# One written list of items from the mixers' result to the second feed-forward, with two blocks 1024 columns wide

## The chip, the core and the metric

The kernel runs on one core of one Trainium2 chip. The metric is the device time in microseconds of one execution; the time of a kernel is the median of its runs. Beside the runs stands one profiled execution, from which every duration here is read.

## The reference

One layer on 256 positions of width 2048, in float32: a SwiGLU feed-forward, two mixers side by side, cross-attention into 256 memory positions with 4 heads of 512, and a second feed-forward. The part that matters here lies in the middle:

```python
y = jnp.concatenate([rms_norm(ya, out_norm_conv[l]), rms_norm(yb, out_norm_sgu[l])], axis=-1)
x = x + y @ w_mix_out[l]
h = rms_norm(x, xattn_norm[l])
mem_n = rms_norm(mem, mem_norm[l])
x = x + memory_cross_attention(h, mem_n, w_q[l], w_kv[l], w_o[l])
h = rms_norm(x, ffn2_norm[l])
x = x + MACARON_SCALE * swiglu_ffn(h, ffn2_w_in[l], ffn2_w_out[l])
```

Inside the attention, `q = h @ w_q`, the scores are `q @ k.T / sqrt(512)`, their softmax is multiplied by the values, and the four heads' outputs, joined, by `w_o`. `w_mix_out`, `w_q` and `w_o` are 2048 x 2048 each. Each residual sum is followed by an RMS norm, so the next product needs a sum of squares over all of `x`; the kernel leaves that factor to the end of the next product and applies only the gain beforehand.

## The kernel before

**Weights.** Every float32 weight is split into two halves of a shorter type. SP's queue loads a tile `raw` of 128 x 1024 (512 KB) from HBM; ScalarE casts it to the high half (L145), VectorE subtracts the high half from `raw` to get the low half (L146). Both halves go into one place `hl`. There are 4 raws (`wraw`) and 3 places (`whl`). TensorE then runs three matmuls for each product: high half of the activations by high half of the weights (L225), by the low half (L226), and low half of the activations by the high half (L227). One tile of weights gives 12 matmuls of 128 x 512.

**The middle, by `gemm_n` (L213).** The mixers' result, the queries and the attention's result are each computed in 4 blocks of 512 columns; a block takes 8 tiles of weights (of two rows of 128 each) and two accumulators. The first halves of the mixers' first two blocks stand earlier, beside the mixers; of the second halves each takes 4 tiles. In what order each engine runs these instructions is set by the framework's scheduler from the order in which the program issues them, with some places tied by hand (`tc.issue_after`).

**A block's way back.** A finished block holds tokens on partitions, but `x` is kept with features on partitions. `by_tokens` (L346) copies the two accumulators out on ScalarE (L350), VectorE transposes in squares of 32 (L388, in `sent`), GpSimd's queue writes the tile to HBM (L390) and, when that has landed, issues four reads back (L393). `arriving` (L353) gives two parts: the first adds the four blocks of features into `x` (`xT`, two additions at L360, which wait for the reads) and then makes, for two of them, the next product's activations with gain in both halves (ScalarE L327, VectorE L328) and the sum of squares (ScalarE L303, VectorE L304); the second part does the other two. The parts are put into a later block's loop over the weights by `between`.

**Heads.** `probabilities` (L1518) splits a head's keys and queries, multiplies them, and runs, for each half of the positions, a chain: maximum (VectorE L1531), scale (L1532), exponential with its sum (ScalarE L1535), reciprocal (VectorE L1536), scale (L1537). `turned` transposes the result on TensorE and splits it and the head's values; `attend` multiplies them into `o_hl`.

**The second feed-forward** is an object with a `Line` (L448): a list of `Item`s, each with a source, a place and a use. The engines' order there is the written one: after item s is used, its place is taken by the cast of the next item that lacks one, the subtract of the item before that one follows, and then the parts in the `post` list of item s run. `begin` is its first 16 items (window 1350.1 to 1394.1 us of the trace), with activations of the attention's residual; `x_turn` (L1630) transposes `x` into two buffers and `x_leaves` (L1638) writes those to HBM (1 MB each) for the end of the kernel; `give` (L785) ends a group of columns.

Of the kernel before, what the change touches and what calls it, by code (L numbers as in the profile page):

```python
# [62 lines left out]


# [32 lines left out]
def layer(ctx: ExitStack, tc: tile.TileContext, a: dict):  # L97
# [248 lines left out]
    def by_tokens(name, acc, flat, back, scales=None):  # L346

        o = flat.rearrange("p (q t n) -> p q t n", q=4, t=2)
        for t in range(2):
            nc.scalar.copy(out=o[:, :, t], in_=by_q(acc[t]))  # L350
        sent(name, flat, back)

# [32 lines left out]
    def sent(name, flat, back, q=None):  # L385

        q = q or nc.gpsimd
        nc.vector.transpose(out=flat, in_=flat)  # L388
        away = dram.tile([4, 32, 4, flat.shape[-1] // 4], F32, name=name)
        q.dma_start(out=away.rearrange("i b q n -> (i b) (q n)"), in_=flat)  # L390
        z = back.rearrange("p (i n) -> p i n", i=4)
        for i in range(4):
            q.dma_start(out=z[32 * i:32 * i + 32], in_=away[:, :, i].rearrange("i b n -> b i n"))  # L393
# [160 lines left out]

    class FeedForward:
# [6 lines left out]
        def __init__(self, stack, tags, name, x_hl, gain, w_in, w_out, patterns, sums, steps, out_s, late):  # L562
# [29 lines left out]
            self.line = Line(  # L592
                [Place(lambda: whl.tile([P, 2, 1024], F32R, name="hl")) for _ in range(3)], []
            )
# [4 lines left out]
        def spared(self):  # L599

            spare = big.tile([P, 8192], F32, name="spare", tag=self.tags[2])
            raws = [spare[:, i * 1024:(i + 1) * 1024] for i in range(6)]
            self.u = [spare[:, 6144 + i * 512:6144 + (i + 1) * 512] for i in range(4)]
            self.raws_summed = [raws.pop() for _ in range(2)]
            self.in_spare = self.fixed(raws)
            self.line.raws.extend([Place(lambda: wraw.tile([P, 1024], F32, name="raw")) for _ in range(4)] + self.in_spare)

        def ahead(self, rules):

            head, more = rules  # L610

            def most(s):
                for j, end in enumerate(self.ends):
                    if s <= end:
                        return min(end + more[j], s + head if j == 0 else 1 << 30)
                return 1 << 30
            return most
# [32 lines left out]
        def sides(self, i):  # L650

            k = 2 * self.spairs[i]
            xg = self.u[2 * (i % 2)].rearrange("p (k t) -> p k t", k=2)
            f = self.u[2 * (i % 2) + 1].rearrange("p (f n) -> p f n", f=4)
            a11, a21, a12, a22 = xg[:, 0, :P], xg[:, 0, P:], xg[:, 1, :P], xg[:, 1, P:]
            form = self.forms[i]

            def scaled():
                for q in range(2):
                    nc.scalar.activation(out=xg[:, q], in_=xT[:, k + q], func=AF.Copy, scale=self.gain(k + q))  # L660

            def summed():
                nc.vector.scalar_tensor_tensor(
# [8 lines left out]
            def parted():  # L672
                split(form[:, :, 0], form[:, :, 1], f)
# [138 lines left out]
        def group(self, j):  # L812
            b = {"begun": set()}
            parts = self.pairs(j, ORDERS.get(j, range(8)), lambda p: self.patterns[j][p] == "S", b)
            p1, u2, u4, u5 = self.u
            self.last_seven[1].now.append(lambda: self.joins_first(b, p1))
            self.last_seven[1].post.append(lambda: self.joins_sevens(b, p1, u2, u4, u5))
            parts[-1][-1].post += [
                lambda: self.joins_eights(b, p1, u2, u4, u5), lambda: self.give(j, (p1, u2), (u4, u5)),
# [158 lines left out]
    def given(ff):  # L978
# [3 lines left out]
        ff.in_x[0].until = ff.ends[NG - 1] - 14  # L982
# [4 lines left out]
    def groups(ff, items):  # L987


        for j in range(1, NG):  # L990
# [8 lines left out]
            if j == NG - 1:  # L999
# [4 lines left out]
                ff.in_ring[0].until = ff.in_ring[1].until = len(items) + flat.index(ff.last_seven[-1])  # L1004
            items += flat
            ff.ends.append(len(items))
        for place in ff.in_spare + ff.in_low:
            place.until = len(items) - 1
        return items

    with ExitStack() as stack:
# [165 lines left out]
        ff.in_high[0].until = rest["until_again"] = len(items) - 1  # L1177
# [27 lines left out]
    with ExitStack() as stack:  # L1205
        with tc.tile_pool(name="mix", bufs=1) as pool:
# [280 lines left out]
            x_hl = gained_tile("S1")  # L1487
            ss = st.tile([P, T], F32, name="ss", bufs=2)
            arrivals = []
            for n in range(4):  # L1490
                if n < 2:
                    acc = gemm_n(a["w_mix_out"][n], y_of, acc=accs[n], between=arrivals, after=0, ks=range(0, 8, 2), first=-1, last=7)
                else:
                    acc = gemm_n(a["w_mix_out"][n], y_of, between=arrivals, after=8)
                if n < 3:
                    flat = pool.tile([P, 4, 2, P], F32, name="o", tag="o", bufs=2).rearrange("p q t n -> p (q t n)")
                else:
                    flat = big.tile([P, 8192], F32, name="last_o", tag="S2")[:, :1024]
                by_tokens(f"x_away{n}", acc, flat, flat)
                arrivals += arriving(4 * n, flat, x_hl, "xattn_norm", ss)  # L1500


        with tc.tile_pool(name="attn", bufs=1) as pool:
            def queries(h, between=None, after=8, step=8):
                acc = gemm_n(a["w_q"][h], lambda k: x_hl[:, k], between=between, after=after, step=step)
                flat = pool.tile([P, 1024], F32, name="q", bufs=2)
                by_tokens(f"q_away{h}", acc, flat, flat)
                return flat

            def halves_by_feature(name, flat):  # L1510
                hl = pool.tile([P, KH, 2, T], F32R, name=name)
                z = flat.rearrange("p (i t k a) -> p i t k a", i=4, t=2, k=4)
                for t in range(2):
                    d = hl[:, :, :, t * P:(t + 1) * P].rearrange("p k two (i a) -> p k two i a", i=4)
                    split(d[:, :, 0], d[:, :, 1], z[:, :, t].rearrange("p i k a -> p k i a"))
                return hl

            def probabilities(h, q):  # L1518
                with tc.issue_after(newest_copy[0].ins):
                    k_hl = halves_by_feature("k_hl", kT[:, h])  # L1520
                    q_hl = halves_by_feature("q_hl", q)
                pr = []
                for t in range(2):
                    acc = pa.tile([P, 2, M], F32, name="aux")
                    s = slice(t * P, (t + 1) * P)
                    for d in range(KH):
                        product_joint(acc, q_hl[:, d, 0, s], q_hl[:, d, 1, s], k_hl[:, d], d == 0, d == KH - 1)
                    e = pool.tile([P, M], F32, name="e", bufs=4)
                    mx = st.tile([P, 1], F32, name="mx", bufs=2)
                    sm = st.tile([P, 1], F32, name="sum", bufs=2)  # L1530
                    nc.vector.reduce_max(out=mx, in_=acc[:, 0], axis=AX.X)  # L1531
                    nc.vector.tensor_scalar(  # L1532
                        out=mx, in0=mx, scalar1=r_t[:, t:t + 1], scalar2=-1.0, op0=ALU.mult, op1=ALU.mult
                    )
                    nc.scalar.activation(out=e, in_=acc[:, 0], func=AF.Exp, scale=r_t[:, t:t + 1], bias=mx, accum_out=sm)  # L1535
                    nc.vector.reciprocal(out=sm, in_=sm)  # L1536
                    nc.vector.tensor_scalar(out=e, in0=e, scalar1=sm, scalar2=None, op0=ALU.mult)  # L1537
                    pr.append(e)
                return pr

            def turned(h, pr):

                p_hl = pool.tile([P, 2, 2, T], F32R, name="p_hl")
                for m in range(2):
                    tp = pa.tile([P, 2, T], F32, name="aux")
                    for t in range(2):
                        state["turned"] = nc.tensor.transpose(
                            out=tp[:, 0, t * P:(t + 1) * P], in_=pr[t][:, m * P:(m + 1) * P], identity=ident
                        )
                    split(p_hl[:, m, 0], p_hl[:, m, 1], tp[:, 0])  # L1550
                v_hl = pool.tile([P, 2, 2, HD], F32R, name="v_hl", bufs=2)
                with tc.issue_after(newest_copy[0].ins):
                    split(v_hl[:, 0], v_hl[:, 1], vv[:, :, h * HD:(h + 1) * HD])
                return p_hl, v_hl

            def attend(h, p_hl, v_hl):
                for d in range(KH):
                    acc = ps.tile([P, 2, 256], F32, name="acc")
                    c = slice(d * P, (d + 1) * P)
                    for m in range(2):  # L1560
                        product_joint(acc, v_hl[:, 0, m, c], v_hl[:, 1, m, c], p_hl[:, m], m == 0, m == 1)
                    split(o_hl[:, h * KH + d, 0], o_hl[:, h * KH + d, 1], acc[:, 0])

            state = {}

# [345 lines left out]
```

## Time and profile before

| | |
|---|---|
| runs | 2050.7, 2053.42, 2051.87 us; median 2051.87 |
| profiled execution | 2049.72 us, of which the span from first to last instruction is 2047.9 |
| granted TensorE clock | 0.996 of full, mean of the span |
| TensorE, VectorE, ScalarE, GpSimd busy | 99%, 87%, 61%, 8% of the span |
| moved | 501.05 MB, mean 245 GB/s |
| the stretch that the change rewrites | from about 1071 us (second halves of the mixers' result) to 1394 us (end of `begin`) |

The busy share of TensorE is a mean over stages; its matmuls overlap, so a busy TensorE may still run below its full rate. A group's row gives busy time and mean of one instruction, then the idle time that stood ahead of it on its engine and what ended it. In a timeline's row the bracket at its end is that idle time. In a row of windows each engine has its busy time in the window and, in brackets, the number of instructions; then the granted clock, the share of time in which the DMA engines were busy, and GB/s.

### The profile page before, as it was taken

How to read it: one execution, taken by the hardware profiler on the slowest of the kernel's cores; microseconds unless marked ns; L12 is line 12 of the kernel's file. 1: busy time of each engine (PE TensorE's matmuls, PEld its weight loads, DVE VectorE, ACT ScalarE, POOL GpSimd, SP SyncE). 2: the span in 40 equal slices, each digit the busy share in tenths (PEclk: the TensorE clock that was granted, in tenths of full speed). 3: DMA queues.
4: the chain of work that ended last, by engine and by line, in shares of the span. 5: the costliest groups of instructions: out<-in, count | busy, mean ns of one | idle time of the engine just before them, and what ended most of it. 6: DMA issues, size and time to landing. Idle time of an engine off the chain costs nothing. (4 is left out here: it accounts for less than half of the span.)

```text
span 2047.9 us, 26059 instructions
## 1 busy us (share of the span) xinstructions
PE 2027.9 (99%) x9004; PEld 1673.6 (82%) x9004; DVE 1785.4 (87%) x2474; ACT 1250.3 (61%) x1605; POOL 157.2 (8%) x240
## 2 busy tenths in 40 slices
PE   9999999999999999999999999999999999999998
PEld 8888888888888888888888788777888888888886
DVE  7999999989898989999876666678999999988997
ACT  7666666656665654444655455556667666655555
POOL 0000000000110011011001110100000010000002
PEclk9999999999999999999999999999999999999999
DMA  9889888989676677677667665688888988896665
GB/s 353 269 257 278 269 272 260 279 250 285 216 265 223 214 255 219 207 232 236 197 199 245 213 204 165 200 270 298 263 265 257 285 269 265 237 304 202 206 221 180
DMA packets 149525, 501.05 MB, mean 245 GB/s; under 512 B 17936, under 2 KB 29840, under 8 KB 148752
## 3 DMA queue, kind: packets, MB, share of 16 engines
q1 hardware_dynamic: 129456, 432.64, 62.5%
q0 software_dynamic: 19360, 66.07, 15.0%
q8 instruction: 70, 1.15, 0.2%
q10 hardware_dynamic: 576, 0.66, 0.1%
q14 instruction: 63, 0.52, 0.1%
HBM read 472.05 MB, written 27.26 MB: 244 GB/s over the span
## 5 line engine op out<-in xcount | busy, mean ns | idle before, releaser
L145 ACT CAST hl<-raw 128x1024 fp32r<-128x1024 f32 x224 | 235.3, 1052 | 234.4 <-PE acc L227 176.5
L146 DVE TENSOR_TENSOR hl<-raw,hl 128x1024 fp32r<-128x1024 f32 x224 | 273.1, 1221 | 96.0 <-ACT hl L145 95.6
L513 ACT CAST hl<-raw 128x1024 fp32r<-128x1024 f32 (+1 forms) x132 | 129.7, 994 | 57.4 <-DVE raw L711 22.4
L488 DVE TENSOR_TENSOR hl<-raw,hl 128x1024 fp32r<-128x1024 f32 (+1 forms) x132 | 151.6, 1155 | 14.0 <-ACT hl L513 11.7
L226 PE MATMUL acc<-hl,x_hl 128*128 128x512 f32 x384 | 150.3, 391 | 0.0
L227 PE MATMUL acc<-hl,x_hl 128*128 128x512 f32 x384 | 149.1, 390 | 0.0
L225 PE MATMUL acc<-hl,x_hl 128*128 128x512 f32 x384 | 134.9, 390 | 1.0 <-ACT x_hl L327 1.0
L226 PE MATMUL acc<-hl,m_hl 128*128 128x512 f32 x256 | 100.6, 393 | 0.0
L227 PE MATMUL acc<-hl,m_hl 128*128 128x512 f32 x256 | 99.6, 389 | 0.0
L513 ACT CAST hl<-sums 128x1024 fp32r<-128x1024 f32 x50 | 52.7, 1053 | 63.2 <-DVE sums L708 57.7
L225 PE MATMUL acc<-hl,m_hl 128*128 128x512 f32 x256 | 90.0, 391 | 0.0
L225 PEld LDWEIGHTS acc<-hl,x_hl 128*128 128x128 f32 x384 | 72.0, 188 | 16.4 <-ACT x_hl L327 1.4
L227 PEld LDWEIGHTS acc<-hl,x_hl 128*128 128x128 f32 x384 | 72.1, 188 | 14.8 <-DVE x_hl L328 0.2
L226 PEld LDWEIGHTS acc<-hl,x_hl 128*128 128x128 f32 x384 | 72.1, 188 | 14.7
L417 PE MATMUL acc<-hl,x_hl 128*128 128x512 f32 x192 | 75.1, 391 | 0.8 <-DVE hl L488 0.6
L416 PE MATMUL acc<-hl,x_hl 128*128 128x512 f32 x192 | 74.9, 390 | 0.0
L417 PE MATMUL acc<-more,x_hl 128*128 128x512 f32 x184 | 71.6, 389 | 0.0
L416 PE MATMUL acc<-more,x_hl 128*128 128x512 f32 x184 | 71.6, 389 | 0.0
L647 POOL DMA_DIRECT2D hl_s<-in_ffn_w_in x36 | 31.7, 879 | 489.7 <-ACT hl_s L645 489.7
L513 ACT CAST hl<-raws_out 128x1024 fp32r<-128x1024 f32 (+1 forms) x53 | 51.9, 985 | 27.5 <-PE acc L419 8.6
L488 DVE TENSOR_TENSOR hl<-raws_out,hl 128x1024 fp32r<-128x1024 f32 (+1 forms) x53 | 61.3, 1159 | 8.0 <-ACT hl L513 7.1
L645 ACT ACTIVATE more<-spare 128x1024 fp32r<-128x1024 f32 x36 | 38.1, 1059 | 43.9 <-PE acc L417 43.9
(674 smaller groups left out, 6172.5 us busy)
## 6 DMA issues: line engine op xcount, KB each, us to landing
spare<-in_ffn_w_in SPq DMA_DIRECT2D x208, 512.0 KB, 6.8
raw<-in_ffn_w_in SPq DMA_DIRECT2D x143, 512.0 KB, 6.9
raw<-in_ffn_w_out SPq DMA_DIRECT2D x90, 512.0 KB, 5.1
raws_out<-in_ffn_w_out SPq DMA_DIRECT2D x68, 512.0 KB, 5.4
hl_s<-in_ffn_w_in POOLq DMA_DIRECT2D x36, 512.0 KB, 7.2
more<-in_ffn_w_in POOLq DMA_DIRECT2D x36, 512.0 KB, 7.5
raw<-in_w_mix_vg SPq DMA_DIRECT2D x32, 512.0 KB, 4.6
raw<-in_w_k SPq DMA_DIRECT2D x32, 512.0 KB, 4.4
```

Of the source, the lines that this page charges most:

```text
L145: newest_copy[0] = nc.scalar.copy(out=hl[:, 0, :size], in_=raw[:, :size])
L146: newest[0] = nc.vector.tensor_tensor(out=hl[:, 1, :size], in0=raw[:, :size], in1=hl[:, 0, :size].bitcast(F32), op=ALU.subtract)
L225: nc.tensor.matmul(acc[t], lhsT=x[:, 0, s], rhs=hi[:, k], start=k0 + k == first, stop=False)
L226: nc.tensor.matmul(acc[t], lhsT=x[:, 0, s], rhs=lo[:, k], start=False, stop=False)
L227: newest_matmul[0] = nc.tensor.matmul(acc[t], lhsT=x[:, 1, s], rhs=hi[:, k], start=False, stop=k0 + k == last)
L416: nc.tensor.matmul(acc[t][g], lhsT=x[:, 0, s], rhs=hi[:, cols[g]], start=(t, g) in first, stop=False)
L417: nc.tensor.matmul(acc[t][g], lhsT=x[:, 0, s], rhs=lo[:, cols[g]], start=False, stop=False)
L488: nc.vector.tensor_tensor(out=hl[:, 1, :n], in0=item.raw[:, :n], in1=hl[:, 0, :n].bitcast(F32), op=ALU.subtract)
L513: nc.scalar.copy(out=item.hl[:, 0, :item.n], in_=item.raw[:, :item.n])
L645: nc.scalar.activation(out=hl[:, 1], in_=raw, func=AF.Copy, scale=-1.0)
L647: nc.gpsimd.dma_start(out=hl[:, 1], in_=self.source(*self.sums_at[at]), accum_op=ALU.add)
```

## The change

The four matrices' work and the heads' steps become items of one `Line`, 88 of them, put ahead of the second feed-forward's items in the same list. Items 0 to 23 are the mixers' result (4, 4, 8 and 8 items for its blocks), 24 to 39 the first two heads' queries as one block 1024 wide with four accumulators, 40 to 55 the other two heads', 56 to 71 the first half of `w_o` 1024 wide, 72 to 87 its other two blocks. An item of a wide block reads one row of 128 by 1024 columns where a narrow one reads two by 512; both are 512 KB and 12 matmuls. The weights `w_q` and `w_o` are laid out for that before the launch.

The scheduler's order is replaced by the written one. Where a returning block is added stands at numbered items: `arrives` puts the first part behind one item and the second behind the next. The heads' steps stand in `HEAD_STEPS`, one row per head, one number per step (keys, queries, probabilities, values, turned, attend). The second feed-forward's object, with its 5 further places for weights, is made behind item 68; four raws in its spare buffer join behind item 87. In `begin` the last two blocks of `w_o` arrive behind its items 0, 1 and 7, 8 (before, only the last one came in `begin`, at 4 and 5); `x_turn` moves from items 6 to 13 to items 9 to 15, `x_leaves(0)` from 11 to 14. Half of `attend`'s accumulators come from the other PSUM pool.

```diff
+HEAD_STEPS = (
+    (45, 46, 47, 48, 50, 52),
+    (50, 51, 52, 53, 55, 57),
+    (55, 57, 58, 59, 61, 63),
+    (62, 63, 64, 65, 66, 67),
+)
...
-            arrivals = []
-            for n in range(4):
-                if n < 2:
-                    acc = gemm_n(a["w_mix_out"][n], y_of, acc=accs[n], between=arrivals, after=0, ks=range(0, 8, 2), first=-1, last=7)
-                else:
-                    acc = gemm_n(a["w_mix_out"][n], y_of, between=arrivals, after=8)
...
-                by_tokens(f"x_away{n}", acc, flat, flat)
-                arrivals += arriving(4 * n, flat, x_hl, "xattn_norm", ss)
+        line = Line(hl_places(), raw_places())
...
+        def wide(w, x_of, accs):
+
+            def use(k):
+                def go(hl):
+                    if not accs:
+                        accs.extend(bank(ps, "acc") for _ in range(4))
+                    x = x_of(k)
                     for t in range(2):
+                        s = slice(t * P, (t + 1) * P)
+                        for g in range(2):
+                            c = slice(g * G, (g + 1) * G)
+                            three(
+                                accs[2 * g + t], (x[:, 0, s], x[:, 1, s]), hl[:, 0, c], hl[:, 1, c], k == 0, k == KD - 1
+                            )
                 return go
+            return [fed(use(k), w[:, k]) for k in range(KD)]
...
+        def goes(name, items, accs, tile=flat_tile):
+            flats = state[name] = []
+            def copies():
+                for i in range(len(accs) // 2):
+                    flats.append(tile(i))
+                    o = flats[i].rearrange("p (q t n) -> p q t n", q=4, t=2)
+                    for t in range(2):
+                        nc.scalar.copy(out=o[:, :, t], in_=by_q(accs[2 * i + t]))
+            def through():
+                for i, away in [(i, leaving(f"{name}_{i}", flat)) for i, flat in enumerate(flats)]:
+                    returned(away, flats[i])
+            items[-1].now.append(copies)
+            items[-1].post.append(through)
+            return items
+        def arrives(at, f, name, i, norm):
+            parts = []
+            def go(q):
+                def part():
+                    if q == 0:
+                        parts.extend(arriving(f, state[name][i], state["x_hl"], norm, state["ss"]))
+                    parts[q]()
+                return part
+            for q in range(2):
+                at[q].post.append(go(q))
...
+        Q, W = 24, 56
+        for at, f, name in ((13, 0, "y_away0"), (18, 4, "y_away1"), (24, 8, "y_away2"), (32, 12, "y_away3")):
+            arrives(items[at:], f, name, 0, "xattn_norm")
+        for at, f, name, i in ((W + 23, 0, "a_away0", 0), (W + 26, 4, "a_away0", 1)):
+            arrives(items[at:], f, name, i, "ffn2_norm")
...
+        for h, steps in enumerate(HEAD_STEPS):
+            for at, part in zip(steps, (keys, asked, probabilities, values, turned, attend)):
+                items[at].post.append(lambda part=part, h=h: part(h))
+        def second():
+            attn.close()
...
-        after = {k: [lambda k=k: x_turn(k - 6)] for k in range(6, 14)}
-        after[4], after[5] = [arrivals[0]], [arrivals[1]]
-        after[11].append(x_leaves(0))
-        after[15] = [x_leaves(1)]
+            after = {k: [lambda k=k: x_turn(k - 9)] for k in range(9, KD)}
...
+            arrives(items, 8, "a_away1", 0, "ffn2_norm")
+            arrives(items[7:], 12, "a_away2", 0, "ffn2_norm")
+            items[14].post.append(x_leaves(0))
+            items[15].post += [lambda: x_turn(7), x_leaves(1)]
...
+        items[W + 12].post.append(second)
```

**How it moves instructions: the third block of the mixers' result on VectorE.** In these rows of VectorE's order `hl` is a tile of weights, `o` the finished block, `xT` the residual `x`. Before:

```order
L388 STREAM_TRANSPOSE o<-o 128x1024
L146 TENSOR_TENSOR hl<-raw,hl 128x1024 x4
L360 TENSOR_TENSOR xT<-xT,o 128x4x128 x2
L146 TENSOR_TENSOR hl<-raw,hl 128x1024
L328 SCALAR_TENSOR_TENSOR x_hl<-xT,pv,x_hl 128x256
L304 TENSOR_TENSOR ss<-ss,sq 128x256
```

After, where line numbers are higher (L496 is the subtract, L392 the transpose, L361 the addition, L336 and L312 the gain and the squares) and every finished block is called `flat`; the rows go from the third block's transpose to its addition, which is the last row but two, and the first addition among them is the second block's:

```order
L392 STREAM_TRANSPOSE flat<-flat 128x1024
L496 TENSOR_TENSOR hl<-raw,hl 128x1024 x3
L361 TENSOR_TENSOR xT<-xT,flat 128x4x128 x2
...
L496 TENSOR_TENSOR hl<-raw,hl 128x1024
...
L496 TENSOR_TENSOR hl<-raw,hl 128x1024 x4
L392 STREAM_TRANSPOSE flat<-flat 128x1024
L496 TENSOR_TENSOR hl<-raw,hl 128x1024
L361 TENSOR_TENSOR xT<-xT,flat 128x4x128 x2
L336 SCALAR_TENSOR_TENSOR x_hl<-xT,pv,x_hl 128x256
L312 TENSOR_TENSOR ss<-ss,sq 128x256
```

Between a block's transpose and its addition stood 4 subtracts; now there are 9, and the next block's transpose.

**The attention's result on VectorE.** Here `h` and `z` are the buffers that hold finished blocks of `w_o`, two each. Before, around the first two blocks:

```order
L388 STREAM_TRANSPOSE h<-h 128x1024
L146 TENSOR_TENSOR hl<-raw,hl 128x1024
L388 STREAM_TRANSPOSE h<-h 128x1024
L146 TENSOR_TENSOR hl<-raw,hl 128x1024 x4
L360 TENSOR_TENSOR xT<-xT,h 128x4x128 x2
L146 TENSOR_TENSOR hl<-raw,hl 128x1024
L328 SCALAR_TENSOR_TENSOR x_hl<-xT,pv,x_hl 128x256 x2
```

After; `ring`, `hl_l` and `hl_h` are the further places for weights:

```order
L392 STREAM_TRANSPOSE h<-h 128x1024 x2
L496 TENSOR_TENSOR hl<-raw,hl 128x1024 x3
L496 TENSOR_TENSOR ring<-raw,ring 128x1024 x2
L496 TENSOR_TENSOR hl_l_10369<-raw,hl_l_10369 128x1024
L496 TENSOR_TENSOR hl_l_10370<-raw,hl_l_10370 128x1024
L496 TENSOR_TENSOR hl_h<-raw,hl_h 128x1024
L392 STREAM_TRANSPOSE z<-z 128x1024
L361 TENSOR_TENSOR xT<-xT,h 128x4x128 x2
L336 SCALAR_TENSOR_TENSOR x_hl<-xT,pv,x_hl 128x256 x2
```

Where 4 subtracts stood between the second transpose and the first addition, there are now 8 and the third block's transpose.

**A head's softmax on VectorE.** `aux` are the scores, `mx` and `sum` their maximum and sum, `e` the probabilities. Before, from the second head's split queries:

```order
L154 TENSOR_TENSOR q_hl<-q,q_hl 128x4x128 x2
L146 TENSOR_TENSOR hl<-raw,hl 128x1024 x2
L388 STREAM_TRANSPOSE q<-q 128x1024
L146 TENSOR_TENSOR hl<-raw,hl 128x1024
L154 TENSOR_TENSOR o_hl<-acc,o_hl 128x256 x4
L1531 TENSOR_REDUCE mx<-aux 128x1 x2
L1532 TENSOR_SCALAR mx<-mx,r_t 128x1 x2
L1536 RECIPROCAL sum<-sum 128x1
L1537 TENSOR_SCALAR e<-e,sum 128x256
L1536 RECIPROCAL sum<-sum 128x1
L1537 TENSOR_SCALAR e<-e,sum 128x256
L146 TENSOR_TENSOR hl<-raw,hl 128x1024 x2
```

After, from the first head's:

```order
L162 TENSOR_TENSOR q_hl<-flat,q_hl 128x4x128 x2
L496 TENSOR_TENSOR hl<-raw,hl 128x1024
L392 STREAM_TRANSPOSE flat<-flat 128x1024
L1655 TENSOR_REDUCE mx<-aux 128x1
L1656 TENSOR_SCALAR mx<-mx,r_t 128x1
L1660 RECIPROCAL sum<-sum 128x1
L1661 TENSOR_SCALAR e<-e,sum 128x256
L1655 TENSOR_REDUCE mx<-aux 128x1
L1656 TENSOR_SCALAR mx<-mx,r_t 128x1
L1660 RECIPROCAL sum<-sum 128x1
L1661 TENSOR_SCALAR e<-e,sum 128x256
L496 TENSOR_TENSOR hl<-raw,hl 128x1024
```

The two halves' chains ran interleaved; now the second starts when the first has ended, and the next subtract stands behind both.

More of the change, by code (lines that the diff above doesn't have):

```diff
@@ L553, in run, with hl_places, raw_places, __init__ @@
                 last[i.engine] = i
+    def hl_places():
+        return [Place(lambda: whl.tile([P, 2, 1024], F32R, name="hl")) for _ in range(3)]
+    def raw_places():
+        return [Place(lambda: wraw.tile([P, 1024], F32, name="raw")) for _ in range(4)]
     class FeedForward:
-        def __init__(self, stack, tags, name, x_hl, gain, w_in, w_out, patterns, sums, steps, out_s, late):
+        def __init__(self, stack, tags, name, x_hl, gain, w_in, w_out, patterns, sums, steps, out_s, late, line=None):
             self.w_in, self.w_out, self.x_hl, self.gain = w_in, w_out, x_hl, gain
@@ L604, in spared @@
             self.raws_summed = [raws.pop() for _ in range(2)]
-            self.in_spare = self.fixed(raws)
-            self.line.raws.extend([Place(lambda: wraw.tile([P, 1024], F32, name="raw")) for _ in range(4)] + self.in_spare)
+            self.spare_raws = raws
+            self.line.raws.extend(self.in_spare)
         def ahead(self, rules):
@@ L612, in most @@
             def most(s):
+                s -= self.base
                 for j, end in enumerate(self.ends):
                     if s <= end:
[L615 removed]
+                        return self.base + min(end + more[j], s + head if j == 0 else 1 << 30)
                 return 1 << 30
@@ L1658, in layer @@
-        items = ff.begin(
-            lambda k: None, after, (r_x, inverse_root_parts(r_x, lambda: x_tot[0][:, 0, 0:2], 1.0 / D, RMS_EPS)), (0, 1, 2, 9),
-        )
-        items[14].post.append(lambda: given(ff))
-        groups(ff, items)
-        rest = {}
-        sums = st.tile([P, 2, 4], F32, name="sums")
-        st.tile([P, 136], F32, name="to_64_too")
-        most = [st.tile([P, 1], F32, name=f"f_most{t}") for t in range(2)]
-        def quarters(o):
-            return [o[:, t, g * G:(g + 1) * G] for g in range(2) for t in range(2)]
@@ L1765, in layer @@
-        items[ff.ends[NG - 1] - 5].post.append(raws_out)
-        items[ff.ends[NG - 1] - 1].post.append(ff.out_places)
-        parts, _, _ = ff.block(0, first_place, lambda o: None)
-        flat = [item for part in parts for item in part]
-        for i in range(6, 2 * NG):
-            flat[i - 6].post.append(ff.turn(i))
-        flat[1].post.append(lambda: ff.by_blocks(NG - 1))
-        flat[2].post.append(lambda: ff.leaves(NG - 1))
-        flat[16].post.append(hl_out)
-        items += flat
@@ new lines, in values, with turned @@
+        def values(h):
+            state["v"] = pool.tile([P, 2, 2, HD], F32R, name="v_hl")
+            split(state["v"][:, 0], state["v"][:, 1], vv[:, :, h * HD:(h + 1) * HD])
+        def turned(h):
+            pr, p_hl = state["p"], pool.tile([P, 2, 2, T], F32R, name="p_hl")
+            for m in range(2):
+                tp = pa.tile([P, 2, T], F32, name="aux")
+                for t in range(2):
+                    nc.tensor.transpose(
+                        out=tp[:, 0, t * P:(t + 1) * P], in_=pr[t][:, m * P:(m + 1) * P], identity=ident
+                    )
+                split(p_hl[:, m, 0], p_hl[:, m, 1], tp[:, 0])
+            state["p_hl"] = p_hl
@@ L1820, in layer @@
+        last = items[-1]
+        items[W + 12].post.append(second)
         line.add(items)
-        line.most = ff.ahead(AHEAD[1])
         line.run()
```

552 lines of the change are left out of this document (280 added, 272 removed).

## The prediction

> **What bounds the kernel now.** I read the page first, then the table of windows for the stretch that the change rewrites, the waits, and the timeline around each gap. The page's line of engines:
>
> ```profile
> PE 2027.9 (99%) x9004; PEld 1673.6 (82%) x9004; DVE 1785.4 (87%) x2474; ACT 1250.3 (61%) x1605; POOL 157.2 (8%) x240
> ```
>
> TensorE sets the time, so only its lost time can be won. The windows, cut where TensorE stood idle and where it didn't (columns: window, its length, PE, PEld, DVE, ACT, POOL busy with their counts, TensorE's clock, DMA share, GB/s):
>
> ```profile
> 1131.40:1138.40 7.00, 3.77 (x11) 2.67 (x10) 5.64 (x10) 4.31 (x10) 0.00 (x0) 0.77 0.25 74
> 1138.40:1158.00 19.60, 19.60 (x87) 16.24 (x86) 11.04 (x12) 8.87 (x10) 2.77 (x5) 1.00 0.84 257
> 1159.40:1316.00 156.60, 156.60 (x788) 133.00 (x789) 97.16 (x143) 82.98 (x128) 16.77 (x30) 1.00 0.65 197
> 1316.00:1323.50 7.50, 5.72 (x18) 4.23 (x17) 7.38 (x14) 6.05 (x14) 0.00 (x0) 0.77 0.39 107
> 1344.60:1350.10 5.50, 3.29 (x14) 2.07 (x12) 5.50 (x11) 4.67 (x10) 0.00 (x0) 1.00 0.31 95
> 1350.10:1394.10 44.00, 44.00 (x195) 36.32 (x196) 38.31 (x60) 25.86 (x39) 2.78 (x5) 1.00 0.88 305
> 1400.90:1408.20 7.30, 5.75 (x17) 3.71 (x16) 6.54 (x9) 5.33 (x7) 0.93 (x1) 0.77 0.75 164
> ```
>
> The second row gives the full rate: 19.60 / 87 = 0.2253 us a matmul, so an item of 12 takes 2.70. A gap's loss is its length less its matmuls at that rate: A (1131) 7.00 - 11 x 0.2253 = 4.5; C (1316) 7.50 - 18 x 0.2253 = 3.4; D (1345) 5.50 - 14 x 0.2253 = 2.3; F (1401) 7.30 - 17 x 0.2253 = 3.5. The waits of TensorE up to 1400 add a small one, B, in the queries' first block:
>
> ```profile
> PE acc L226 <- DVE hl L146: 6.6, 3, 3.2
> PE acc L225 <- ACT x_hl L327: 1.0, 1, 1.0
> PE acc L417 <- DVE hl L488: 0.6, 1, 0.6
> ```
>
> (total, times, longest.) So A to D cost 4.5 + 1.0 + 3.4 + 2.3 = 11.2, F another 3.5. TensorE waits for the subtract; the timelines of VectorE and TensorE at A show what that waited for:
>
> ```profile
> 1124.52 1.23 DVE L146 TENSOR_TENSOR hl<-raw,hl 128x1024 fp32r<-128x1024 f32 x1 [1.50 <-ACT hl L145]
> 1132.76 1.29 DVE L360 TENSOR_TENSOR xT<-xT,o 128x512 f32<-128x512 f32 x2 [7.01 <-DMA o<-x_away]
> 1133.97 1.22 DVE L146 TENSOR_TENSOR hl<-raw,hl 128x1024 fp32r<-128x1024 f32 x1
> 1131.39 0.61 PE L225 MATMUL acc<-hl,y_hl 128*128 128x512 f32 x2
> 1135.24 0.80 PE L226 MATMUL acc<-hl,y_hl 128*128 128x512 f32 x1 [3.23 <-DVE hl L146]
> 1135.84 0.63 PE L227 MATMUL acc<-hl,y_hl 128*128 128x512 f32 x1
> ```
>
> VectorE stood 7.01 us at an addition whose block had not come back, with the next subtract behind it; 1.2 us after that subtract began, TensorE went on, with wider spacing for a while. The same addition opens C, D, and, in `begin`, the backlog ahead of F:
>
> ```profile
> 1316.12 1.29 DVE L360 TENSOR_TENSOR xT<-xT,h 128x512 f32<-128x512 f32 x2 [5.56 <-DMA h<-o_away]
> 1344.11 1.29 DVE L360 TENSOR_TENSOR xT<-xT,z 128x512 f32<-128x512 f32 x2 [5.35 <-DMA z<-o_away]
> 1371.08 1.29 DVE L360 TENSOR_TENSOR xT<-xT,z 128x512 f32<-128x512 f32 x2 [4.90 <-DMA z<-o_away]
> ```
>
> **The change part by part.** An item is 12 matmuls of 128 x 512, one 512 KB load, one cast and one subtract in either form, so TensorE's work and the bytes stay; what can change is the gaps.
>
> *The returns come in time (gains A to D).* GpSimd's rows of the first write of a return, for A, C, D and the last block:
>
> ```profile
> 1117.54 0.56 POOL L390 DMA_DIRECT2D x_away<-o  x1 [15.92 <-DVE o L388]
> 1299.90 0.56 POOL L390 DMA_DIRECT2D o_away<-h  x1 [50.05 <-DVE h L388]
> 1329.90 0.56 POOL L390 DMA_DIRECT2D o_away<-z  x1 [15.27 <-DVE ss L304]
> 1353.52 0.56 POOL L390 DMA_DIRECT2D o_away<-z  x1 [15.13 <-DVE z L388]
> ```
>
> To the additions above these are 15.2, 16.2, 14.2 and 17.6 us. Only 4 subtracts stood between, some 4 x 2.70 = 10.8 us, which is why each addition waited. Now the distance from a block's last item to the item behind which it is added is 10, 11, 9 and 9 items for the mixers' result, 8 and 11 for the wide block of `w_o`, 9 and 8 for the narrow ones. From these go the copies out and the transpose:
>
> ```profile
> L350 ACT COPY q<-acc 128x512 f32<-128x512 f32 x8 | 4.6, 588 | 5.4 <-PE acc L227 5.1
> L388 DVE STREAM_TRANSPOSE q<-q 128x1024 f32<-128x1024 f32 x4 | 5.0, 1245 | 4.6 <-ACT q L350 4.6
> ```
>
> 2 x 0.59 + 1.25 and some handing over, 2.6 us. The shortest narrow allowance is 8 x 2.70 - 2.6 = 19.0. The wide one has two more copies ahead of its first write, so at worst 8 x 2.70 - 2.6 - 1.2 = 17.8, against 16.2 for the pair of blocks in C, and 17.6 is the longest return seen. Tight there, ample elsewhere. GpSimd's queue holds a second block's reads behind the first's as before. I take the whole 11.2; the bounds are nothing (all late again) and 11.2.
>
> The clock's part in these losses: TensorE's granted clock is 0.77 in A after 3.23 us idle, but also in C, after 7.50 - 5.72 = 1.8. The Trainium skill, TensorE: Matmul & The Clock Gate, Part 1, says that the clock falls to half after at least one idle window of about 3.4 us. By that page a gap would cost only its idle time, A to D 3.23 + 1.0 + 1.8 + 2.2 = 8.2 and F 1.55, the gain here would be some 4 smaller, near 2044; the rows of C and F, with clock 0.77 after under 2 us idle, disagree, and the measured losses stand.
>
> *The written order adds work between a tile's release and its subtract.* With 3 places, the subtract of item s+3 has from the end of item s to the end of s+2, 2 x 2.70 = 5.4 us, and what is posted behind item s stands ahead of it on VectorE. The rows:
>
> ```profile
> L146 DVE TENSOR_TENSOR hl<-raw,hl 128x1024 fp32r<-128x1024 f32 x87 | 105.9, 1220 | 64.5 <-ACT hl L145 64.5
> L328 DVE SCALAR_TENSOR_TENSOR x_hl<-xT,pv,x_hl 128x256 fp32r<-128x256 f32 x32 | 14.6, 480 | 0.6 <-ACT x_hl L327 0.6
> L304 DVE TENSOR_TENSOR ss<-ss,sq 128x256 f32<-128x256 f32 x30 | 12.6, 419 | 0.3
> ```
>
> An arrival's first part is 1.29 + 2 x 0.48 + 2 x 0.42 = 3.1; with the subtract's 1.22, 4.3 of 5.4. It fits by 1.1 if the block is there; a late one comes on top. The second part is shorter.
>
> *A head's chain.* Rows of its steps:
>
> ```profile
> L1531 DVE TENSOR_REDUCE mx<-aux 128x1 f32<-128x256 f32 x8 | 3.3, 414 | 1.5 <-PE aux L161 1.5
> L1532 DVE TENSOR_SCALAR mx<-mx,r_t 128x1 f32<-128x1 f32 x8 | 1.5, 211 | 0.1
> L1535 ACT ACTIVATE e<-aux,mx,r_t 128x256 f32<-128x256 f32 x8 | 4.5, 564 | 8.3 <-DVE mx L1532 8.3
> L1535 ACT ACTIVATION_READ_ACCUMULATOR e<-aux,mx,r_t 128x1 f32 x8 | 1.6, 194 | 0.0
> L1536 DVE RECIPROCAL sum<-sum 128x1 f32<-128x1 f32 x8 | 1.3, 162 | 1.4 <-ACT e L1535 1.2
> L1537 DVE TENSOR_SCALAR e<-e,sum 128x256 f32<-128x256 f32 x8 | 2.8, 353 | 0.2
> ```
>
> One half is 0.41 + 0.21 + 0.56 + 0.19 + 0.16 + 0.35 = 1.9. The scores are 24 matmuls of 256 columns; from the attention's window, (156.60 - 580 x 0.2253) / 208 = 0.125 each (the four heads have 192 such matmuls and 16 transposes, which leaves 580 of the 788 at 512 columns), so 3.0 us, the first half done at 1.5. The chain ends at 1.5 + 1.9 + 1.9 = 5.3, the subtract behind it at 6.5. Item s+3 starts at 3.0 + 5.4 = 8.4. Some eight handings over between engines at 0.1 to 0.2 (1.2 us for eight ahead of the reciprocal) leave about 1 us. The next two items carry the values' split and stay within it too, by less. Before, this window had no idle time at all (156.60 of 156.60), so there is nothing to win and I can only lose: between 0 and, by 0.3 at each of eight places, 2.4; I take 1.2, the middle, as the margin is of the size of the handings over.
>
> *The opening of the second feed-forward (F).* Of `begin`'s 44.0 us VectorE was busy 38.31 and stood 4.9 at the late addition; the backlog ran into F. Now the third block's arrival is in `begin` too, 1.29 + 4 x (0.48 + 0.42) = 4.9 more; the five further places let up to five subtracts, 6.1, be done before it, and the wait of 4.9 goes if the returns hold. That is 38.3 + 4.9 - 6.1 = 37.1 of 44, without a wait. I take 2.5 of F's 3.5; bounds -3.5 (as much again lost) and 3.5. `x_leaves(0)` moves three items later in SP's queue, past three loads, to the end of item 14, 2.7 before `begin` ends; it has landed 6.2 later, and `give`, which overwrites its source, came 5.4 after `begin`'s end:
>
> ```profile
> x_away<-h SPq DMA_DIRECT2D x1, 1024.0 KB, 6.2
> 1399.53 1.40 DVE L795 SCALAR_TENSOR_TENSOR h<-acc,r_x,h 128x512 f32<-128x512 f32 x2
> ```
>
> So 2.7 + 5.4 = 8.1 for 6.2, hidden by 1.9; the transposes that it waits for are posted two items before. Moving `x_turn` changes no work. Counted at nothing; without that cover, up to 6.2, which is in the second case below.
>
> Sum, against the profiled execution: -11.2 - 2.5 + 1.2 = -12.5, so 2049.72 - 12.5 = 2037.2. The median of the runs, 2051.87, is 2.15 above the profiled one; 2037.2 + 2.15 = **2039.4**.
>
> **The rivals.** *VectorE binds in the opening.* If the places fill late (raws from the spare buffer come only behind item 87), the 6.1 isn't done ahead: 38.3 + 4.9 = 43.2 of 44, and F doubles instead of going. -11.2 + 1.2 + 3.5 = -6.5: 2045.4. For it: VectorE is the second engine, 87% busy. Against: nothing holds the five casts back before item 87 but raws, of which four circulate.
>
> *Slower: subtracts late behind the softmax.* Written in order, a chain that waits for TensorE and twice for ScalarE keeps the weights' subtract waiting, where the scheduler had interleaved the halves. If chain and subtract take longer than 8.4 rather than 6.5 plus handing over, each head loses at two places about 1.0 of wait and, as in A, 3.77 - 11 x 0.2253 = 1.3 of low clock: 4 x 2 x 2.3 = 18.4. -11.2 - 2.5 + 18.4 = +4.7: 2056.6. For it: the addition at A shows one late instruction on VectorE stopping TensorE. The same page of the Trainium skill, Architectural detail, says that VectorE's and ScalarE's queues are strict FIFO, TensorE's alone reorders, its weight loads; A agrees. Against: 1.9 us of room by the rows.
>
> *It doesn't do what it says.* The longer distances are eaten by slower returns, as two blocks now leave together and loads run beside them; A and C survive in part at new places (4.5 + 3.4 kept, and a new 2): -12.5 + 7.9 + 2 = -2.6: 2049.3, no change. For it: returns vary from 14.2 to 17.6, the worst beside the fullest DMA (0.88). Against: most allowances are over 21.
>
> **How the numbers follow.** Forecast 0.60; more still (all 14.7 of A to F with no new gap, 2037.2) 0.06; opening 0.18; no change 0.10; slower 0.06. A measurement here can tell about 0.2%, 4.1 us, from no change, so up to 2047.8 counts as faster: 0.60 + 0.06 + 0.18 = 0.84; same 0.10; slower 0.06. The range runs from the best case less the 2.7 by which the three runs differ, rounded up, 2035, to the opening's case and as much of that scatter beyond it as stays short of no change, 2047; it leaves out the last two cases, 0.16.
>
> **What would show it.** Right: no window with TensorE idle at the mixers' result and at `w_o`; the additions' waits for reads near zero; VectorE's waits moved to casts. Attention's window as long per matmul as before, with waits for the subtract (line 496) under 0.5 each. The opening without a window at clock 0.77. Wrong: an addition waiting over 1 us with a subtract behind it; TensorE waiting for `hl` within attention by over 2 us in all; `give` waiting for a DMA.

## The result and the profile after

The changed kernel takes 2033.95 us (median of 4 runs, 2033.29 to 2034.6), the one before in the same measurement 2052.64 (4 runs, 2050.7 to 2058.6): a ratio of 0.9904, 95% interval 0.9883 to 0.9925; the medians differ by 18.7 us. Faster, as forecast, by more than forecast: 2039.4 was predicted, and the range ended at 2035.0, 1.05 above what was measured.

The page of the changed kernel, its engines and the first line of its chain:

```profile
PE 2022.1 (99%) x9004; PEld 1670.5 (82%) x9004; DVE 1786.8 (88%) x2474; ACT 1251.5 (62%) x1605; POOL 156.7 (8%) x240
PE 91%; DVE 3%; DMA 3%; issue 1%; ACT 1%; POOL 0%; SPq 0%; ACTq 0%; DVEq 0%; POOLq 0%
```

The work is the same in number. TensorE now has 91% of the chain that the page follows back from the last instruction (38% before). All waits of TensorE from 1020 to 1440 us, of the changed kernel:

```profile
PE acc L425 <- DVE ring L496: 0.2, 1, 0.2
```

One wait of 0.2 us is left; before, the same answer had five rows with 9.8 us. Why is seen at the additions. Before, VectorE stood idle ahead of them for 27.9 us (what was waited for, us in all, times):

```profile
DMA z<-o_away: 10.3, 2
DMA o<-x_away: 9.8, 3
DMA h<-o_away: 5.6, 1
DMA last_o<-x_away: 2.2, 1
```

After (line 361 now), the answer lists the additions and then, under the heading on idle time, what they waited for:

```profile
L361 DVE TENSOR_TENSOR xT<-xT,flat x8: 679/686/687, 1110.6 to 1162.9; 128x512 f32<-128x512 f32 x8
L361 DVE TENSOR_TENSOR xT<-xT,h x4: 648/682/685, 1318.2 to 1326.9; 128x512 f32<-128x512 f32 x4
L361 DVE TENSOR_TENSOR xT<-xT,z x4: 681/686/691, 1341.1 to 1358.5; 128x512 f32<-128x512 f32 x4
its engine sat idle before it (us, times) until:
who waited for it (us, times):
```

Nothing stands under that heading: no addition found its block missing. The returns themselves are no faster: from the issue of the write to the landing of the last read they take 8.5 to 17.5 us in the trace before and 10.0 to 18.2 after. Seven of the eight additions start 4.8 us or more after their block has landed, the last one only 0.2 us (landed at 1357.67, started at 1357.87).

The time by stage, from windows cut at the first matmul of each. Before: the mixers' result, queries to attention's result, `begin`:

```profile
1049.40:1141.90 92.50, 89.14 (x385) 73.06 (x384) 56.28 (x70) 46.48 (x66) 8.32 (x15) 0.98 0.69 212
1141.90:1349.00 207.10, 202.75 (x982) 170.01 (x980) 130.83 (x190) 110.24 (x173) 22.31 (x40) 0.99 0.66 202
1349.00:1394.10 45.10, 44.46 (x197) 36.41 (x196) 39.41 (x61) 26.96 (x41) 2.78 (x5) 1.00 0.86 302
```

After:

```profile
1051.00:1138.10 87.10, 87.10 (x386) 72.10 (x385) 52.42 (x60) 44.37 (x59) 8.30 (x15) 1.00 0.75 231
1138.10:1338.00 199.90, 199.90 (x981) 169.16 (x980) 138.44 (x196) 115.50 (x178) 22.16 (x40) 1.00 0.69 217
1338.00:1382.20 44.20, 44.20 (x197) 36.45 (x196) 41.42 (x71) 30.85 (x50) 2.77 (x5) 1.00 0.80 271
```

The mixers' result takes 5.4 us less, queries to attention's result 7.2, `begin` 0.9. The rest behind `begin`, where gap F was, takes 2047.9 - 1394.1 = 653.8 before and 2032.7 - 1382.2 = 650.5 after, 3.3 less. Ahead of the change the profiled execution after is 1.6 slower (the first window starts at 1051.0 against 1049.4). Together 5.4 + 7.2 + 0.9 + 3.3 - 1.6 = 15.2, the whole difference of the spans.

### The profile page after: what moved, and what is told of

The parts are those of the page before. It is cut to its first block, busy times and chain, and to the rows that moved or that the text cites. A ratio compares the mean times of both kernels' runs of the same rounds, so it can differ in the third digit from the quotient of the medians.

```text
span 2032.7 us, 26057 instructions
## 1 busy us (share of the span) xinstructions
PE 2022.1 (99%) x9004; PEld 1670.5 (82%) x9004; DVE 1786.8 (88%) x2474; ACT 1251.5 (62%) x1605; POOL 156.7 (8%) x240
## 3 DMA queue, kind: packets, MB, share of 16 engines
q0 software_dynamic: 19360, 66.07, 15.2%
## 4 chain that ended last, share of the span: by engine, by line
PE 91%; DVE 3%; DMA 3%; issue 1%; ACT 1%; POOL 0%; SPq 0%; ACTq 0%; DVEq 0%; POOLq 0%
PE acc L425 13%; PE acc L424 13%; PE acc L427 13%; PE acc L412 10%; PE acc L411 10%; PE acc L413 10%; PE acc L235 5%; PE acc L234 5%; PE acc L233 5%; PE aux L412 2%; PE aux L411 2%; PE aux L413 2%; DMA raw<-in_ffn_w_in 1%; DVE hl L496 1%; DMA o<-g_away 1%
## 5 line engine op out<-in xcount | busy, mean ns | idle before, releaser
L521 ACT CAST hl<-raw 128x1024 fp32r<-128x1024 f32 (+1 forms) x216 | 215.6, 1006 | 148.5 <-PE acc L413 63.4
L496 DVE TENSOR_TENSOR hl<-raw,hl 128x1024 fp32r<-128x1024 f32 (+1 forms) x216 | 250.8, 1168 | 59.4 <-ACT hl L521 57.1
L153 ACT CAST hl<-raw 128x1024 fp32r<-128x1024 f32 x136 | 142.7, 1051 | 140.3 <-PE acc L235 94.9
L154 DVE TENSOR_TENSOR hl<-raw,hl 128x1024 fp32r<-128x1024 f32 x136 | 166.1, 1223 | 31.3 <-ACT hl L153 31.1
L234 PE MATMUL acc<-hl,x_hl 128*128 128x512 f32 x256 | 100.4, 392 | 0.1
L235 PE MATMUL acc<-hl,x_hl 128*128 128x512 f32 x256 | 99.7, 389 | 0.0
L233 PE MATMUL acc<-hl,x_hl 128*128 128x512 f32 x256 | 89.4, 390 | 0.1
L521 ACT CAST hl<-sums 128x1024 fp32r<-128x1024 f32 x46 | 48.4, 1053 | 51.7 <-DVE sums L727 45.2
L411 PE MATMUL acc<-hl,x_hl 128*128 128x512 f32 x202 | 78.9, 391 | 0.0
L412 PE MATMUL acc<-hl,x_hl 128*128 128x512 f32 x202 | 78.8, 390 | 0.0
L413 PE MATMUL acc<-hl,x_hl 128*128 128x512 f32 x202 | 78.6, 389 | 0.0
L425 PE MATMUL acc<-hl,x_hl 128*128 128x512 f32 x188 | 73.6, 391 | 0.1
L424 PE MATMUL acc<-hl,x_hl 128*128 128x512 f32 x188 | 73.4, 390 | 0.0
L496 DVE TENSOR_TENSOR hl<-spare,hl 128x1024 fp32r<-128x1024 f32 (+1 forms) x52 | 57.0, 1099 | 4.7 <-ACT hl L521 3.6
L521 ACT CAST hl<-spare 128x1024 fp32r<-128x1024 f32 (+1 forms) x52 | 48.4, 950 | 20.5 <-DVE spare L730 13.3
```

The lines of the kernel that those rows point to most:

```text
L154: newest[0] = nc.vector.tensor_tensor(out=hl[:, 1, :size], in0=raw[:, :size], in1=hl[:, 0, :size].bitcast(F32), op=ALU.subtract)
L233: nc.tensor.matmul(acc[t], lhsT=x[:, 0, s], rhs=hi[:, k], start=k0 + k == first, stop=False)
L234: nc.tensor.matmul(acc[t], lhsT=x[:, 0, s], rhs=lo[:, k], start=False, stop=False)
L235: newest_matmul[0] = nc.tensor.matmul(acc[t], lhsT=x[:, 1, s], rhs=hi[:, k], start=False, stop=k0 + k == last)
L411: nc.tensor.matmul(acc, lhsT=x[0], rhs=hi, start=first, stop=False)
L412: nc.tensor.matmul(acc, lhsT=x[0], rhs=lo, start=False, stop=False)
```

## The experiments

The theory is distance: what counts is how many items lie between a block's departure and its addition on VectorE, because the return takes some 10 to 19 us in these traces and everything behind a waiting addition waits too (the subtract at A). Rivals: the written list itself, the wide blocks, or the places filled ahead.

### The list kept, the distance undone

```diff
-        for at, f, name in ((13, 0, "y_away0"), (18, 4, "y_away1"), (24, 8, "y_away2"), (32, 12, "y_away3")):
+        for at, f, name in ((8, 0, "y_away0"), (12, 4, "y_away1"), (20, 8, "y_away2"), (28, 12, "y_away3")):
...
-        for at, f, name, i in ((W + 23, 0, "a_away0", 0), (W + 26, 4, "a_away0", 1)):
+        for at, f, name, i in ((W + 20, 0, "a_away0", 0), (W + 22, 4, "a_away0", 1), (W + 28, 8, "a_away1", 0)):
...
-            arrives(items, 8, "a_away1", 0, "ffn2_norm")
-            arrives(items[7:], 12, "a_away2", 0, "ffn2_norm")
+            arrives(items[4:], 12, "a_away2", 0, "ffn2_norm")
```

> The changed kernel with every addition put back near its block: behind item 8, 12, 20, 28 for the mixers' result (1, 5, 5, 5 items after the blocks' last ones: 5 for the first, 5, 5, 5 counting from items 3, 7, 15, 23), 5 and 7 items behind the wide block of the attention's result, 5 behind each narrow one. Theory 1, distance: a return took 14 to 18 us and now has 5 x 2.7 - 2.6 = 11, so each addition waits 3 to 7 us on VectorE with the subtract behind it; with 3 places for weights TensorE stops 1 to 5 us at the additions of the mixers' result, and less at the attention's result, where 8 places are filled ahead: 2039 to 2048 us. Rival, the written list itself: the order and the places did it and the distance is spare, 2034 to 2036.

Measured: 2053.56 us, ratio to the kernel before 1.0003 (0.9989 to 1.0017). The whole gain is gone, more than the expectation said. What its additions waited for (28.0 us in all, where the kernel before had 27.9), and what TensorE waited for from 1020 to 1440:

```profile
DMA z<-a_away: 12.6, 2
DMA flat<-y_away: 9.6, 4
DMA h<-a_away: 5.8, 1
PE acc L425 <- DVE hl_l L496: 8.2, 2, 5.7
PE acc L412 <- DVE hl L496: 4.9, 5, 1.8
PE acc L425 <- DVE ring L496: 2.4, 1, 2.4
```

So list, wide blocks and places without the distance are worth nothing in the sum. They do move the loss: from first matmul to first matmul the mixers' result and the attention take 90.7 and 202.7 us (92.5 and 207.1 before), but `begin` takes 56.5 (45.1 before). The expectation that places filled ahead would cover the attention's result failed there: the two longest waits of TensorE (8.2) stand in `begin`, where VectorE lost 12.6 us to the last two blocks.

### The distance alone, under the scheduler

The kernel before, with its parts put into later blocks' loops and tied behind the newest subtract. Without that tie the built program has the additions of the mixers' result among the same subtracts as before, although the loops ask for later places. `x_turn` and `x_leaves(0)` also stand where the change has them; those lines and some small ones are left out here.

```diff
             if between and k0 >= after and k0 % step == 0:
-                between.pop(0)()
+                with tc.issue_after(newest[0].ins):
+                    between.pop(0)()
...
-                    acc = gemm_n(a["w_mix_out"][n], y_of, acc=accs[n], between=arrivals, after=0, ks=range(0, 8, 2), first=-1, last=7)
+                    acc = gemm_n(a["w_mix_out"][n], y_of, acc=accs[n], ks=range(0, 8, 2), first=-1, last=7)
-                    acc = gemm_n(a["w_mix_out"][n], y_of, between=arrivals, after=8)
+                    acc = gemm_n(a["w_mix_out"][n], y_of, between=arrivals if n == 2 else None, after=8)
...
-                between=arrivals, after=8,
+                between=arrivals if n == 3 else None, after=8,
```

> The kernel before, scheduler and narrow blocks kept, with only the additions (and, behind them, x_turn) put later: 7 subtracts instead of 4 between the third block's transpose and its addition, 11 instead of 4 for the attention's first, 8 to 9 for its last two. The fourth block's addition keeps its 5, as the first block of queries needs it. Theory 1, distance: gaps A, C and D go, the wait at the fourth block (B) stays or grows to 3 us: 8 to 13 us faster than before, 2039 to 2044. Rival, the written list: under the scheduler other waits take their place, less than 4 us faster.

Measured: 2038.21, ratio 0.9934 (0.9912 to 0.9956), some 14 of the 18 us. TensorE's waits, same window:

```profile
PE acc L225 <- ACT x_hl L328: 1.2, 1, 1.2
PE acc L418 <- DVE hl L489: 1.1, 1, 1.1
PE aux L1651 <- DVE ss L305: 0.4, 1, 0.4
```

A, C and D are gone. B stays at 1.2, as it should: its distance was left as it was. The opening keeps two waits. The distance, nearly alone, carries most of the gain; the remaining 4 us came only with the changed kernel, and which of its parts brings them was not taken apart.

### The queries narrow

```diff
-        items += goes("q_away0", wide(a["w_q_wide"], of("x_hl"), accs[0]), accs[0])
-        for n in range(2):
-            items += goes(f"q_away{n + 1}", narrow(a["w_q"][n], of("x_hl"), accs[1 + n]), accs[1 + n])
+        for n in range(4):
+            qs = accs[(0, 1, 2, 6)[n]]
+            items += goes(f"q_away{n}", narrow(a["w_q"][n], of("x_hl"), qs), qs)
...
-        for at, f, name in ((13, 0, "y_away0"), (18, 4, "y_away1"), (24, 8, "y_away2"), (32, 12, "y_away3")):
+        for at, f, name in ((13, 0, "y_away0"), (18, 4, "y_away1"), (24, 8, "y_away2"), (28, 12, "y_away3")):
```

> The changed kernel with the queries as four blocks 512 wide instead of one of 1024 and two of 512. The first block reaches the last four features at its seventh item instead of the thirteenth, so the fourth block of the mixers' result is added 5 items after its end instead of 9. Theory 1: that return needs 14 to 18 us and has 11; a gap of 2 to 6 us opens at the start of the queries and nothing else changes: 2036 to 2040. Rival: the width is for nothing but fewer blocks, 2033 to 2035.

Measured: 2034.95, ratio 0.9913 (0.9887 to 0.9939); the changed kernel's 2033.95 lies inside its scatter (2033.25 to 2035.63). The expected gap did not open, and no wait of TensorE is listed. GpSimd's row of the departure and VectorE's of the addition:

```profile
1142.11 0.56 POOL L394 DMA_DIRECT2D y_away<-flat  x1 [11.79 <-DVE flat L392]
1152.95 1.29 DVE L361 TENSOR_TENSOR xT<-xT,flat 128x512 f32<-128x512 f32 x2
```

This block was back within 10.8 us, without a wait. The returns that took 14 to 18 were others; I had put their price on this one too. The margin is thin: the block had landed about 1 us before its addition, and the same return took 12.6 in the kernel before and 13.9 in the near list. At the queries the width buys nothing that these runs can measure. The wide block of `w_o` was not tried narrow: its first half would need the last head at the seventh item, before that head is done.

### No places filled ahead

```diff
-                    return self.base + min(end + more[j], s + head if j == 0 else 1 << 30)
+                    return self.base + min(end + more[j], s + (head if s >= 0 else 3) if j == 0 else 1 << 30)
```

> The changed kernel with the five further places for weights held back: before the second feed-forward's first item no more than 3 items are made ahead, as elsewhere in the list, instead of 6. Theory A: the casts and subtracts made ahead, up to three items more, are what keeps VectorE clear in the opening, gap F comes back: 2 to 6 us slower, 2036 to 2040. Theory B: F came from the late addition alone, which is gone: 2033 to 2035.

Measured: 2040.23, ratio 0.9934 (0.991 to 0.9957), 6.3 us slower than the changed kernel. TensorE's waits:

```profile
PE aux L1619 <- DVE ss L312: 2.6, 1, 2.6
PE acc L425 <- DVE ring L496: 2.3, 1, 2.3
PE acc L412 <- DVE hl_l L496: 0.7, 1, 0.7
```

The opening needs both: the additions in time and the subtracts made ahead. Theory A holds in place and, at the edge of its range, in size: the wait for `ring` stands where F had been, and between 1401 and 1408 us TensorE loses 4.1 us, against F's 4.0 (counted from start to start, as below). That agrees with the second case of the prediction, VectorE binding without this work done ahead. But not all of the 6.3 us can be put down to it: the last block's return took 19.6 us in this run, its addition waited 2.5 us for it, and the wait of 2.6 for `ss` follows behind that.

### The softmax chain made longer

One and six more scalings by 1.0 behind each half's scaling:

```diff
                 nc.vector.tensor_scalar(out=e, in0=e, scalar1=sm, scalar2=None, op0=ALU.mult)
+                for _ in range(6):
+                    nc.vector.tensor_scalar(out=e, in0=e, scalar1=1.0, scalar2=None, op0=ALU.mult)
```

In the changed kernel, the end of a head's chain on VectorE and the subtract behind it:

```profile
1209.87 0.35 DVE L1661 TENSOR_SCALAR e<-e,sum 128x256 f32<-128x256 f32 x1
1210.14 1.22 DVE L496 TENSOR_TENSOR hl<-raw,hl 128x1024 fp32r<-128x1024 f32 x1
1212.20 0.39 PE L411 MATMUL acc<-hl,x_hl 128*128 128x512 f32 x1
1212.42 0.39 PE L412 MATMUL acc<-hl,x_hl 128*128 128x512 f32 x1
```

It ends at 1210.14 + 1.22 = 1211.36; the item that needs it starts on TensorE at 1212.20, 0.8 later. The expectations take this 0.8. The first matmul of an item uses the high half, though, which the cast makes; the second (last row) is the first to need the subtract, 1.1 later.

> The changed kernel with one more scaling by 1.0 of each half's probabilities on VectorE: two instructions of 0.35 us a head, 0.27 from start to start, 0.54 us in all ahead of the subtract. In the changed kernel's trace the subtract behind the first head's chain ended 0.8 us before TensorE needed it. Theory, a margin of 0.8: no gap, within 1 us of 2034. Rival, the order has eaten the room: 0.5 us and a low clock at each of 8 places, 2040 or more.

Measured: 2034.39, ratio 0.992 (0.9899 to 0.9941): no difference, and no wait of TensorE listed.

> The same with six more scalings of each half: twelve instructions a head, 3.2 us ahead of the subtract. Theory, a margin of 0.8: each head's subtract is 2.4 us late, 4 x 2.4 = 9.7 and, with a low clock of 1.3 behind some of them, up to 15: 2043 to 2049. Rival, there is slack that the sum did not see (TensorE's scores or a later item take it up): 2034 to 2037.

Measured: 2046.39, ratio 0.9972 (0.9961 to 0.9983), 12.4 more. TensorE's waits:

```profile
PE acc L412 <- DVE hl L496: 6.9, 4, 2.9
PE aux L1675 <- DVE e L1663: 0.8, 1, 0.8
```

Four waits for the subtract, one per head, the longest 2.9 where 3.2 - 0.8 = 2.4 was expected. The slower rival was a real mechanism: 0.5 us more cost nothing, 3.2 us more cost two thirds of the gain.

### Nearer by two items

```diff
-        for at, f, name in ((13, 0, "y_away0"), (18, 4, "y_away1"), (24, 8, "y_away2"), (32, 12, "y_away3")):
+        for at, f, name in ((11, 0, "y_away0"), (15, 4, "y_away1"), (22, 8, "y_away2"), (30, 12, "y_away3")):
...
-        for at, f, name, i in ((W + 23, 0, "a_away0", 0), (W + 26, 4, "a_away0", 1)):
+        for at, f, name, i in ((W + 21, 0, "a_away0", 0), (W + 24, 4, "a_away0", 1), (W + 30, 8, "a_away1", 0)):
...
-            arrives(items, 8, "a_away1", 0, "ffn2_norm")
-            arrives(items[7:], 12, "a_away2", 0, "ffn2_norm")
+            arrives(items[5:], 12, "a_away2", 0, "ffn2_norm")
```

> The changed kernel with the additions nearer by about two items: 8, 8, 7 and 7 items behind the mixers' blocks, 6 and 9 behind the wide block of the attention's result, 7 and 6 behind its narrow ones. Allowances 16.3 and more for the mixers' result, 12.4 to 16.3 for the other. Returns in the traces took 10 to 15 us in the first place and 14 to 18 in the second. So nothing at the mixers' result; at the attention's result waits of 1 to 4 us on VectorE, of which the places filled ahead hide most: 2034 to 2039. Rival, the distance must be what it is: over 2040.

Measured: 2042.37, ratio 0.9955 (0.9939 to 0.9971). The theory's range, to 2039, is missed; the time is the rival's, over 2040. GpSimd's row of the last block's departure and VectorE's of its addition:

```profile
1344.93 0.56 POOL L394 DMA_DIRECT2D a_away<-z  x1 [15.36 <-DVE x_hl L336]
1363.76 1.29 DVE L361 TENSOR_TENSOR xT<-xT,z 128x512 f32<-128x512 f32 x2 [6.98 <-DMA z<-a_away]
```

This return took 18.8 us, and 7 us of VectorE's time in `begin` went with it; the first block of the attention's result was late too, by 3.7 us. Most of TensorE's waits, none over 1.2 us, follow in the opening; the mixers' result, with 16 us and more, has no waiting addition, though TensorE waits there once, 0.7 us, for a subtract. The places hide less than I had expected. Two items decide 8 us, most of them behind `w_o`: there the distances of the change are not far above what is needed, while at the mixers' result its additions have 7 us and more to spare.

## Why the prediction was right in kind and wrong in size

**The mechanism** was right: late returns made A, C, D and the backlog at F, and longer distances removed them. Both directions of the test show it, the near list (0 us left) and the far scheduler (14 us). One step of it held by luck: the shortest narrow allowance was put at 19.0 us, but the last block had 17.4 (written from 1340.50, added at 1357.87), and its return took 17.2.

**A to D were mis-sized: 11.2 predicted.** By the stages 5.4 + 7.2 + 0.9 = 13.5 came back. The step that failed is "a gap's loss is its length less its matmuls at that rate". A window's count holds matmuls that began before it. TensorE's timeline of the kernel before shows it at C, whose window begins at 1316.00: the first two rows belong to matmuls counted in it, so 16 and not 18 start there.

```profile
1315.76 0.39 PE L226 MATMUL acc<-hl,o_hl 128*128 128x512 f32 x1
1315.99 0.39 PE L227 MATMUL acc<-hl,o_hl 128*128 128x512 f32 x1
1316.21 0.61 PE L225 MATMUL acc<-hl,o_hl 128*128 128x512 f32 x2
1318.61 0.50 PE L226 MATMUL acc<-hl,o_hl 128*128 128x512 f32 x1 [1.78 <-DVE hl L146]
1319.41 0.54 PE L227 MATMUL acc<-hl,o_hl 128*128 128x512 f32 x1
1319.75 0.63 PE L225 MATMUL acc<-hl,o_hl 128*128 128x512 f32 x1
1321.88 0.63 PE L227 MATMUL acc<-hl,o_hl 128*128 128x512 f32 x1
1322.31 1.37 PE L225 MATMUL acc<-hl,o_hl 128*128 128x512 f32 x4
```

Some rows in between are left out. The better sum takes each matmul's start to the next one's start, less what undisturbed starts lie apart (0.2268 us for 512 columns: 1315.76 to 1315.99, for one; for narrower ones the median of their kind). So counted, A lost 5.1, B 1.3, C 3.7, D 2.8, together 12.9, which is 1.7 more than predicted; F 4.0. Another 0.4 stands in the mixers' result and 0.8 in the attention. The attention's window with 156.60 busy of 156.60 was read as free of loss; matmuls of 0.39 us that start every 0.23 overlap, and a late start inside that overlap leaves no idle time. This matters little: most of that 0.8 is still there after the change (0.6). By the same count the stretch loses 18.5 in all before and 1.7 after: a difference of 16.8, as the stages give (5.4 + 7.2 + 0.9 + 3.3). The range failed by the same step: its best case had 14.7 to win where 16.8 came back.

**New gaps behind the chains: 1.2 predicted, none measured.** The margin of about 1 us was right (1.1 by the trace, at the first head), but the middle of the bounds was taken although the sum said that it fits. With it the forecast was 1.2 too slow.

**F: 2.5 predicted, 3.3 measured** by the windows. Its reason holds: with the places held back the loss at F returns. Its working does not: VectorE was to be busy 37.1 of 44 us in `begin` and was busy 41.4 of 44.2.

**The clock.** Taking the measured losses, low clock included, was right: at C the starts lie 0.43 us apart after an idle time of 1.78. The Trainium skill, TensorE: Matmul & The Clock Gate, Part 1, has the clock at half after at least one idle window of about 3.4 us. From that rule the prediction worked out a time near 2044; the rows at C disagree with the rule, and the measured 2033.95 lies on the other side of the forecast.

**The step from the profiled execution to the median: 2.15 predicted.** After the change it is 2033.95 - 2034.45 = -0.5. The profiled execution of the kernel before was ahead by 1.0 to 3.3 us when the mixers' result began (1049.4, against 1050.4 to 1052.7 in the eight other traces), so this part of the offset was real. Some 1 us is left, for which no run shows a cause: the kernel before varies by 8 us within one measurement, the changed one by 1.3.

Sum of the misses: 13.5 - 10.0 = 3.5 for A to D less the gaps expected (1.7 by the gaps' size, 1.2 by the new gaps, 0.6 by scattered losses that went too), 0.8 for F, 2.15 + 0.5 - 1.6 = 1.05 for the offset: 5.35 of the 5.45 us. No single term carries it; all of them erred to the same side.

**The rivals.** The opening bound by VectorE didn't happen, because the places do fill ahead. The slower chain didn't happen, by about 1 us. "Slower returns" didn't happen, but at the last block by 0.2 us only.

## What to carry to other kernels

An addition that waited for its read held up the subtract behind it on VectorE (7.01 us at A), so the place of the wait mattered more than the transfer: count the items between departure and use, times the item's length, and hold it against the longest round trip in the trace at that stage. Where the scheduler leaves the wait too near, tie it behind a later instruction of the same engine, or write the order. And size a gap by start to start of the matmuls, not by a window's idle time or count.

## What the runs showed of the hardware that I had not expected

- The granted clock fell after less than 2 us of idle time at C, but not after every such gap: at C TensorE stood 1.78 us, ran on at full rate for some 0.9 us (1318.61 to about 1319.5), and only then at half rate, 0.43 us from start to start, until about 1322.9 (rows above). At D it stood 1.57 us, and the clock stayed full. The three low phases in this stretch of the trace before, at A, C and F, lasted 3.4 us each (1135.2 to 1138.6, 1319.5 to 1322.9, 1404.8 to 1408.2).
- Round trips of 512 KB out and back took very different times: at most 10.8 us at the start of the queries, 18.8 beside the loads of the second feed-forward.
- Kernels with late returns scatter more: runs of the near list lie between 2050.2 and 2057.1, of the changed kernel between 2033.3 and 2034.6. That the transfers cause the scatter was not tested.
